# A row softmax on one core: the sixth load split in 14 and 2 rows, and the first store issued when the 14 rows have landed

## The chip, the cores and the metric

The kernel runs on one core of a Trainium2 chip. The metric is the device time of one execution in microseconds (us). The core has a vector engine (DVE), a scalar engine (ACT), a general engine (POOL) and a queue engine (SP), and 16 DMA engines that move data between the device memory (HBM) and the core's own memory. A DMA is issued by an instruction on the queue of ACT, SP or POOL, and each of the 16 DMA engines carries out its share of it. In the profile the DMA queue of ACT is called q10, that of SP q1 and that of POOL q0.

## The reference

The input is 16 x 1024 rows of 512 float32 numbers. Each row is divided by 0.5 and put through a softmax with the usual shift by the row's maximum:

```python
x_scaled = x / 0.5
x_max = np.max(x_scaled, axis=-1, keepdims=True)
exp_x = np.exp(x_scaled - x_max)
return exp_x / np.sum(exp_x, axis=-1, keepdims=True)
```

33.55 MB are read and 33.55 MB are written.

## The kernel before

The 16384 rows are cut in 8 chunks of 4 MB. A chunk is a tile of 128 partitions with 16 rows each, so one row index g (0 to 15) stands for 128 rows, and one partition's part of a chunk is 32 KB in one piece. Six chunk buffers exist (`BUFS`); chunks 6 and 7 reuse the buffers of chunks 0 and 1. All work is done in place.

A chunk is worked on in blocks (`BLOCKS`): chunk 0 in three (4, 4 and 8 rows), chunk 7 in two (8 and 8), all others whole. For each block there are four steps:

- `shift` (L74, L78): DVE takes the negative maximum of each row and doubles it. The result is the bias.
- `exponentials` (L104): ACT takes exp(2x + bias), one instruction for each row index, with the row's sum read out beside it.
- `scale_vector` (L121, L123): DVE inverts the sums and multiplies all row indices but the last eighth.
- `scale_scalar` (L134): ACT multiplies the last eighth (2 row indices of 16, 1 of 8).

The order on every engine is the order in which the program is written. The main loop goes over the blocks. For block i it issues the exponentials of block i+1, then the two scaling steps of block i, then the shift of block i+2, then the store of block i's chunk if the block is the chunk's last one. For chunk 1 the last two exponentials come after that store (function `rows`).

The loads (L65) of chunks 0 to 5 are all issued on ACT's queue at the start, one behind the other: chunk 0 in two pieces, the others whole. Chunks 6 and 7 are loaded on SP's queue. Load 6 waits until the store of chunk 0 has landed, load 7 until that of chunk 1 has; the last two rows of chunk 7 are loaded by POOL (L93), behind a small copy (L87) that waits for an exponential of chunk 5. All eight stores (L144) are issued on ACT's queue, each for a whole chunk of 4 MB. So loads 0 to 5 and all stores share one queue, and a store that is issued while loads are still under way lies behind them. At the end SP waits for all transfers.

Of the kernel before, what the change touches and what calls it, by code (L numbers as in the profile page):

```python
# [1 line left out]

# [4 lines left out]


@with_exitstack
def kernel(  # L10
    ctx: ExitStack,
    tc: tile.TileContext,
    x: bass.AP,
    out: bass.AP,
):
    nc = tc.nc
    fp32 = mybir.dt.float32
    P = nc.NUM_PARTITIONS
    AX = mybir.AxisListType.X
    EXP = mybir.ActivationFunctionType.Exp  # L20
    COPY = mybir.ActivationFunctionType.Copy
    MAX = mybir.AluOpType.max

    D = x.shape[-1]
    xf = x.flatten_outer_dims()
    of = out.flatten_outer_dims()
    N = xf.shape[0]

    G = 16
    C = N // (P * G)
    assert C * P * G == N
    xr = xf.rearrange("(c p g) d -> c p g d", p=P, g=G)
    outr = of.rearrange("(c p g) d -> c p g d", p=P, g=G)
    WHOLE = [(0, G)]
    LATE = 2
    LOADS = [[(0, 4), (4, G)]] + [WHOLE] * 6 + [[(0, G - LATE)]]
    BLOCKS = [[(0, 4), (4, 8), (8, G)]] + [WHOLE] * 6 + [[(0, 8), (8, G)]]  # L40
    STORES = [WHOLE] * 8
    BMAX = 16
    BUFS = 6

    data = ctx.enter_context(tc.tile_pool(name="data", bufs=BUFS))
    stats = ctx.enter_context(tc.tile_pool(name="stats", bufs=6))

    ctx.enter_context(tc.manual_schedule())


    chunks = {}
    blocks = [(c, lo, hi) for c in range(C) for lo, hi in BLOCKS[c]]
    n = len(blocks)
    biases, sums, recips = {}, {}, {}

    finished = []
    def load(c):
        if c < BUFS:
            chunks[c] = data.tile([P, G, D], fp32, name="xt")
        else:  # L60
            chunks[c] = chunks[c - BUFS]
        xt = chunks[c]
        queue = nc.scalar if c < BUFS else nc.sync
        for lo, hi in LOADS[c]:
            part = queue.dma_start(out=xt[:, lo:hi, :], in_=xr[c][:, lo:hi, :])  # L65
            finished.append(part.ins.name)

    def shift(i):
        c, lo, hi = blocks[i]
        if c not in chunks:  # L70
            load(c)
        b = hi - lo
        negmax = stats.tile([P, BMAX], fp32, name="negmax")
        nc.vector.tensor_reduce(  # L74
            negmax[:, 0:b], chunks[c][:, lo:hi, :], axis=AX, op=MAX, negate=True
        )
        biases[i] = stats.tile([P, BMAX], fp32, name="bias")
        nc.vector.tensor_scalar_mul(biases[i][:, 0:b], negmax[:, 0:b], 2.0)  # L78

    def load_last_rows(signal):
        seen = stats.tile([P, 1], fp32, name="seen", bufs=1)
        copied = nc.gpsimd.tensor_copy(out=seen, in_=signal)  # L87
        finished.append(copied.ins.name)
        c = C - 1
        to = chunks[c - BUFS][:, G - LATE : G, :]  # L90
        of_ = xr[c][:, G - LATE : G, :]
        for p0, p1 in ((P - 2, P), (0, P - 2)):
            part = nc.gpsimd.dma_start(  # L93
                out=to[p0:p1], in_=of_[p0:p1], max_dma_last_dim=4 * D
            )
            finished.append(part.ins.name)

    def exponentials(i, rows):
        c, lo, hi = blocks[i]
        if i not in sums:  # L100
            sums[i] = stats.tile([P, BMAX], fp32, name="sums")
        for g in rows:
            row = chunks[c][:, lo + g, :]
            nc.scalar.activation(  # L104
                out=row,
                in_=row,
                func=EXP,
                bias=biases[i][:, g : g + 1],
                scale=2.0,
                accum_out=sums[i][:, g : g + 1],  # L110
            )
            if c == BUFS - 1 and g == 10:
                load_last_rows(sums[i][:, g : g + 1])


    def scale_vector(i):
        c, lo, hi = blocks[i]
        b = hi - lo
        k = b - b // 8
        recips[i] = stats.tile([P, BMAX], fp32, name="recip")  # L120
        nc.vector.reciprocal(recips[i][:, 0:b], sums[i][:, 0:b])  # L121
        rows = chunks[c][:, lo : lo + k, :]
        last = nc.vector.tensor_mul(  # L123
            rows, rows, recips[i][:, 0:k].unsqueeze(2).broadcast_to((P, k, D))
        )
        if i == n - 1:
            finished.append(last.ins.name)

    def scale_scalar(i):
        c, lo, hi = blocks[i]  # L130
        b = hi - lo
        for g in range(b - b // 8, b):
            row = chunks[c][:, lo + g, :]
            last = nc.scalar.activation(  # L134
                out=row, in_=row, func=COPY, scale=recips[i][:, g : g + 1]
            )
            if i == n - 1:
                finished.append(last.ins.name)

    def store(i):  # L140
        c, _, end = blocks[i]
        for lo, hi in STORES[c]:
            if hi == end:
                part = nc.scalar.dma_start(  # L144
                    out=outr[c][:, lo:hi, :], in_=chunks[c][:, lo:hi, :]
                )
                if c < C - 1:
                    finished.append(part.ins.name)

    load(0)  # L150
    warm = stats.tile([P, 1], fp32, name="warm", bufs=1)
    nc.vector.memset(warm, 0.0)  # L152
    nc.scalar.activation(out=warm, in_=warm, func=EXP)  # L153
    for c in range(1, BUFS):
        load(c)

    shift(0)
    shift(1)

    def rows(i):  # L160
        c, lo, hi = blocks[i]
        cut = hi - lo - (2 if c == 1 else 0)
        return range(cut), range(cut, hi - lo)

    exponentials(0, rows(0)[0])
    for i in range(n):
        if i + 1 < n:
            exponentials(i + 1, rows(i + 1)[0])
        scale_vector(i)
        scale_scalar(i)  # L170
        if i + 2 < n:
            shift(i + 2)
        store(i)
        if i + 1 < n:
            exponentials(i + 1, rows(i + 1)[1])

    seen = nc.sync.nop()
    info = mybir.DependencyInfo(
        mybir.DependencyClass.Sync, mybir.DependencyReason.DATA
    )  # L180
    for name in finished:
        tc.add_manual_dep(seen.ins, name, info, reason="leaves one wait for the end")


# [1 line left out]
_INS = ['x']  # L186
_OUTS = [((16, 1024, 512), 'float32')]


# [23 lines left out]
```

## Time and profile before

| what | us |
|---|---|
| median of 3 runs | 162.73 (162.13 to 162.80) |
| the profiled execution | 162.08 |
| its span, first to last instruction | 160.2 |
| DVE busy | 134.6 |
| ACT busy | 102.2 |
| store of chunk 0 issued | 44.16 |
| store of chunk 1 issued | 59.02 |
| load 6 issued by SP | 72.61 |
| load 7 issued by SP | 88.3 |
| last multiply of DVE ends | 147.5 |
| last store issued | 147.56 |

All times inside the run count from the start of the span. The page's row named DMA gives the mean busy share of the 16 DMA engines in 40 slices of 4 us, a 9 being 90% or more; "busy" counts the time that packets took, so an engine with slow packets is busy too. In the groups of issues, the last number is the time from a DMA's issue to its landing, which includes the time that it lies behind others in its queue. In a table of stretches a line has the stretch, its length, the busy time of DVE, ACT and POOL with the number of instructions in brackets, the clock, the DMA share and the GB/s moved by the packets that started in it. In a timeline a line has start, duration, engine, line of the program, operation, tiles, and in square brackets the idle time before it and what ended it.

### The profile page before, as it was taken

Reading aid. Unit: us, or ns where it says so; the run is one execution under the profiler, and the core shown is the slowest. Engines: PE = TensorE matmul, PEld = TensorE weight load, DVE = VectorE, ACT = ScalarE, POOL = GpSimd, SP = SyncE. Lnnn points to the kernel's source line nnn. Section 1 sums busy time; section 2 is a strip of 40 time slices with the busy share of each in tenths; the row PEclk is TensorE's granted clock in tenths of the full one; section 3 lists DMA queues with packets and bytes.
Section 4 is the critical chain, followed back from the end, with each engine's and each line's share of the span. In section 5 each row is a group of like instructions: output and inputs, shape, how many; then the busy total and the mean of one; then the engine's idle time right before and its main releaser. Section 6 shows DMA issues by size and latency. Waiting matters only on the chain.

```text
span 160.2 us, 410 instructions
## 1 busy us (share of the span) xinstructions
DVE 134.6 (84%) x45; ACT 102.2 (64%) x273; POOL 1.9 (1%) x7
## 2 busy tenths in 40 slices
DVE  0607999999999999999999999999999999958000
ACT  3071549069989972998199909991899891690000
POOL 0000000000000000000000000040000000000000
DMA  5999999999999997999999999999999999999995
GB/s 184 470 401 507 401 393 499 417 393 468 442 401 442 466 401 303 475 393 434 475 401 417 475 409 417 444 459 394 428 456 436 397 466 450 393 442 466 401 401 245
DMA packets 2642, 67.13 MB, mean 419 GB/s; under 512 B 336, under 2 KB 336, under 8 KB 464
## 3 DMA queue, kind: packets, MB, share of 16 engines
q10 hardware_dynamic: 2160, 58.72, 86.0%
q1 hardware_dynamic: 288, 7.86, 11.4%
q0 software_dynamic: 192, 0.52, 0.8%
q14 instruction: 2, 0.02, 0.0%
HBM read 33.55 MB, written 33.55 MB: 419 GB/s over the span
## 4 chain that ended last, share of the span: by engine, by line
DVE 76%; DMA 7%; issue 5%; ACT 3%; ACTq 0%
DVE negmax L74 42%; DVE xt L123 32%; DMA xt<-in_x_dram 7%; ACT xt L104 3%; DVE bias L78 1%; DVE recip L121 1%; ACTq L65 0%
## 5 line engine op out<-in xcount | busy, mean ns | idle before, releaser
L104 ACT ACTIVATE xt<-xt,bias 128x512 f32<-128x512 f32 x128 | 90.4, 708 | 40.7 <-DVE bias L78 39.8
L74 DVE TENSOR_REDUCE negmax<-xt 128x16 f32<-128x8192 f32 (+2 forms) x11 | 69.9, 6353 | 9.5 <-DMA xt<-in_x_dram 9.5
L123 DVE TENSOR_TENSOR xt<-xt,recip 128x7168 f32<-128x7168 f32 (+2 forms) x11 | 62.0, 5637 | 0.4
L104 ACT ACTIVATION_READ_ACCUMULATOR xt<-xt,bias 128x1 f32 x128 | 23.9, 187 | 0.0
L134 ACT ACTIVATE xt<-xt,recip 128x512 f32<-128x512 f32 x15 | 9.9, 706 | 0.0
L121 DVE RECIPROCAL recip<-sums 128x16 f32<-128x16 f32 (+2 forms) x11 | 2.4, 219 | 1.8 <-ACT xt L104 1.8
L153 ACT ACT_TABLE_LOAD x1 | 1.3, 1283 | 1.6 <-PEq L197 1.6
L78 DVE TENSOR_SCALAR bias<-negmax 128x16 f32<-128x16 f32 (+2 forms) x11 | 1.9, 173 | 0.4
L93 POOL DMA_DIRECT2D xt<-in_x_dram x2 | 1.5, 741 | 0.5 <-issue 0.5
L87 POOL COPY seen<-sums 128x1 f32<-128x1 f32 x1 | 0.2, 184 | 103.7 <-ACT xt L104 103.7
L152 DVE MEMSET warm<- 128x1 f32 x1 | 0.1, 59 | 0.8 <-PEq L197 0.8
L153 ACT ACTIVATE warm<-warm 128x1 f32<-128x1 f32 x1 | 0.2, 202 | 0.0
L197 POOL MEMSET const-bfloat16-1.0<- 128x1 bf16 x1 | 0.1, 96 | 0.0
L197 POOL MEMSET const-uint8-127<- 128x1 uint8 x1 | 0.1, 96 | 0.0
L197 POOL MEMSET const-float32-0.0<- 128x1 f32 x1 | 0.1, 93 | 0.2 <-issue 0.2
L197 POOL MEMSET const-float32-1.0<- 128x1 f32 x1 | 0.1, 93 | 0.0
## 6 DMA issues: line engine op xcount, KB each, us to landing
out_dram<-xt ACTq DMA_DIRECT2D x8, 4096.0 KB, 24.9
xt<-in_x_dram ACTq DMA_DIRECT2D x5, 4096.0 KB, 39.5
xt<-in_x_dram SPq DMA_DIRECT2D x1, 4096.0 KB, 23.6
xt<-in_x_dram SPq DMA_DIRECT2D x1, 3584.0 KB, 26.4
xt<-in_x_dram ACTq DMA_DIRECT2D x1, 3072.0 KB, 11.7
xt<-in_x_dram ACTq DMA_DIRECT2D x1, 1024.0 KB, 4.8
xt<-in_x_dram POOLq DMA_DIRECT2D x1, 504.0 KB, 20.9
xt<-in_x_dram POOLq DMA_DIRECT2D x1, 8.0 KB, 9.6
```

The costliest lines, as they stand in the source:

```text
L74: nc.vector.tensor_reduce(negmax[:, 0:b], chunks[c][:, lo:hi, :], axis=AX, op=MAX, negate=True)
L78: nc.vector.tensor_scalar_mul(biases[i][:, 0:b], negmax[:, 0:b], 2.0)
L87: copied = nc.gpsimd.tensor_copy(out=seen, in_=signal)
L93: part = nc.gpsimd.dma_start(out=to[p0:p1], in_=of_[p0:p1], max_dma_last_dim=4 * D)
L104: nc.scalar.activation(out=row, in_=row, func=EXP, bias=biases[i][:, g : g + 1], scale=2.0, accum_out=sums[i][:, g : g + 1],)
L121: nc.vector.reciprocal(recips[i][:, 0:b], sums[i][:, 0:b])
L123: last = nc.vector.tensor_mul(rows, rows, recips[i][:, 0:k].unsqueeze(2).broadcast_to((P, k, D)))
L134: last = nc.scalar.activation(out=row, in_=row, func=COPY, scale=recips[i][:, g : g + 1])
L152: nc.vector.memset(warm, 0.0)
L153: nc.scalar.activation(out=warm, in_=warm, func=EXP)
L197: nc = _bacc.Bacc("TRN2", target_bir_lowering=False, num_devices=1)
```

## The change

The load of chunk 5, the sixth, is issued as two DMAs: rows 0 to 13 and rows 14 to 15. The store of chunk 0 is issued later in ACT's order: no longer after the scaling of chunk 0's last block, but in the next turn of the loop, just ahead of the store of chunk 1, so behind the exponentials of chunk 2 and the two scaling rows of chunk 1. It is given a wait for the first piece of load 5, the 14 rows. The two exponentials of chunk 1 that stood behind that store are issued with the other fourteen, ahead of chunk 0's scaling row. Nothing else is changed: DVE, POOL and SP have the same instructions in the same order.

```diff
     LATE = 2
-    LOADS = [[(0, 4), (4, G)]] + [WHOLE] * 6 + [[(0, G - LATE)]]
+    TAIL = 2
+    LOADS = [[(0, 4), (4, G)]] + [WHOLE] * 4 + [[(0, G - TAIL), (G - TAIL, G)], WHOLE, [(0, G - LATE)]]
...
     finished = []
+    released_by = {}
+    data_wait = mybir.DependencyInfo(
+        mybir.DependencyClass.Sync, mybir.DependencyReason.DATA
+    )
     def load(c):
...
             finished.append(part.ins.name)
+            released_by.setdefault(c, part.ins.name)
...
                 part = nc.scalar.dma_start(
                     out=outr[c][:, lo:hi, :], in_=chunks[c][:, lo:hi, :]
                 )
+                if c == 0:
+                    tc.add_manual_dep(
+                        part.ins, released_by[BUFS - 1], data_wait,
+                        reason="the first store starts where the loads end",
+                    )
...
     def rows(i):
         c, lo, hi = blocks[i]
-        cut = hi - lo - (2 if c == 1 else 0)
+        cut = hi - lo
         return range(cut), range(cut, hi - lo)
...
         if i + 2 < n:
             shift(i + 2)
-        store(i)
+        if blocks[i][0] == 1:
+            store(i - 1)
+        if blocks[i][0] > 0:
+            store(i)
```

## The prediction

> **What bounds the kernel now.** I read the page first (shares, DMA queues, chain of waits), then the stretches of equal length, then the waits of the SP queue, then the landing times and packet records at the two ends of the run. The page:
>
> ```profile
> DVE 134.6 (84%) x45; ACT 102.2 (64%) x273; POOL 1.9 (1%) x7
> ...
> DMA  5999999999999997999999999999999999999995
> ...
> q10 hardware_dynamic: 2160, 58.72, 86.0%
> q1 hardware_dynamic: 288, 7.86, 11.4%
> q0 software_dynamic: 192, 0.52, 0.8%
> ...
> HBM read 33.55 MB, written 33.55 MB: 419 GB/s over the span
> ...
> DVE 76%; DMA 7%; issue 5%; ACT 3%; ACTq 0%
> ```
>
> Two things are almost always busy: the 16 DMA engines (86.0 + 11.4 + 0.8 = 98% of the span) and DVE, which the chain puts at 76%. The chain follows DVE up to its last multiply; after it, at 147.47, comes the last store, issued at 147.56. So the question is whether that store finds the DMA engines free. The packet records say no for 15 of 16 engines: they end the store before at 148.85 to 149.33 and go on at once; one engine ran dry at 147.59 and began the last store at 148.40. So the DMA engines set the end, and DVE is under 1 us behind them. The rate in stretches of 9.7 us (the time of one 4 MB chunk; the last two columns are the DMA share and GB/s):
>
> ```profile
> 41.40:51.10 9.70, 9.63 (x4) 8.97 (x25) 0.00 (x0) 1.00 1.00 432
> 51.10:60.80 9.70, 9.70 (x2) 7.89 (x22) 0.00 (x0) 1.00 1.02 392
> 60.80:70.50 9.70, 9.63 (x4) 7.50 (x21) 0.00 (x0) 1.00 0.99 429
> 70.50:80.20 9.70, 9.63 (x5) 5.69 (x15) 0.00 (x0) 1.00 1.00 432
> ```
>
> The engines are busy throughout but move only 392 where 432 is usual: 9.7 x 40/432 = 0.9 us lost, in the stretch where the sixth load ends and the first store begins. The packets name it: 32 KB takes 1.21 to 1.22 us everywhere else; the last two packets of the sixth load on each engine take 1.2 to 1.8 and then 1.9 to 2.4. Its sixteen semaphore increments come at 61.66 to 62.78, those of the fifth load at 51.18 to 51.98; earlier loads are 9.71 apart, so 61.69 was due and the load is 1.09 late. Behind it in the same queue lies the first store, issued long before:
>
> ```profile
> 44.16 0.35 ACTq L144 DMA_DIRECT2D out_dram<-xt  x1
> ...
> 57.68 1.32 ACT L134 ACTIVATE xt<-xt,recip 128x512 f32<-128x512 f32 x2
> 59.02 0.35 ACTq L144 DMA_DIRECT2D out_dram<-xt  x1
> 62.79 0.17 DVE L78 TENSOR_SCALAR bias<-negmax 128x16 f32<-128x16 f32 x1
> ...
> 63.00 0.72 ACT L104 ACTIVATE xt<-xt,bias 128x512 f32<-128x512 f32 x1 [4.00 <-DVE bias L78]
> ```
>
> The reader sees here also that ACT, done at 59.4, idles 4.00 us before it can go on at 63.00. Who waits for that store is SP alone:
>
> ```profile
> SPq L65 <- DMA out_dram<-xt: 74.8, 2, 59.6
> ```
>
> **The change, part by part.** All against the profiled execution: span 160.2, time 162.08, so 1.9 us lie around the span. The median of the runs shown is 162.73, 0.65 above it; I apply the difference to the median.
>
> *One more load issue on ACT.* A load issue takes 0.48 us (median on that queue). It lies near 4.3, after the six others; ACT waits for its first bias until 8.09. Nothing, unless that 3 us cover went. The two-row packets are 4 KB: in the POOL load such a packet takes 0.159, so eight on each engine take 1.27, against 1.213 for the same 32 KB: +0.06, plus a 0.009 semaphore packet. Counted below.
>
> *Two exponentials of chunk 1 before the scaling row of chunk 0.* Two by 0.707 = 1.41 later for the scaling row: it would end at 43.43 + 1.41 + 0.70 = 45.5. The next bias comes at 46.34 in either case. Cost nothing; DVE's reciprocal of chunk 1 waits behind its own reduction (to 46.15) anyway. If DVE were 1 us earlier, this would show.
>
> *The first store moves behind the third chunk's exponentials and scaling rows.* ACT comes to it where it issued the second store before, at 59.02. Its issue (0.35) just moves, and the two stores now go one after the other.
>
> *The new wait, for the 14 rows.* The store's start decides. Undisturbed, the whole load is due at 61.69; the 14 rows 1.27 earlier, 60.42. From a landing to the issue that waits for it: 0.10 (first store landed 72.51, SP issued at 72.61). So the issue is at 60.52. From issue to first packet on a dry engine: 0.84 (147.56 to 148.40). First store packets at 61.36 on all engines. ACT stands still 59.02 to 60.52; behind the wait are the second store (60.87 to 61.22) and the exponentials of chunk 3, which need 63.00: 1.8 us of cover. The issue latency is seen once, on one engine of 16, so I bound it: below, 0 (the store's packets wait ready at the moment of issue); above, 1.02, the very first load (0.74 to 1.76). I take 0.84, the only store among these rows.
>
> *What goes, and what is late next.* The stretch should go, since no store lies behind the load while its last packets run; a dry gap comes instead: the 2 rows end about 60.5 to 61.3, so engines stand dry for 0 to 0.9 us. Before, the first store packets stood at 61.34 to 61.99 on fifteen engines (mean 61.70) and 62.48 on the last. At 61.36 for all, the mean engine gains 0.34, the latest of the fifteen 0.63, the earliest nothing. The engines are then full until the last store, so each carries its shift to the end. The engine of 62.48 is no matter: one engine has 1.3 us less to do later. Last packets end between 158.15 and 159.01; the end moves by 0.34 if the late engines at the end are average ones, by 0.63 if they are those late at 61.99. The POOL rows fall unevenly on the engines and mix the order, so I take 0.35.
>
> *SP's sixth-buffer chain.* The first store lands 1.0 us earlier (61.36 + 9.71 + 0.4 = 71.5), so load 6 is issued at 71.6 instead of 72.61. It landed at 96.2 and DVE wants it at 103.94; load 7 at 114.7, wanted at 120.56; POOL's rows at 126.5, wanted at 132.91. Nothing, with 6 us of cover. DVE's order is unchanged, its end stays at 147.47. Sum: -0.35 + 0.
>
> A rule that speaks against the change: the page "DMA: Bandwidth & Descriptors" of the Trainium skill (section "Anatomy of one DMA — SWDGE (gpsimd) path") sets about 2.0 us of fixed setup and completion on each DMA, for GpSimd's path. The rows above give 0.45 from last packet to landing on the slow engine, 0.10 and 0.84, 1.39 in all, from ACT's queue. By the rule the store would come 0.6 later and the sum would be +0.25, or 163.0.
>
> **The floor.** DVE sets how much can be gained: the last store cannot begin before 147.56 + 0.84 = 148.40, against a mean of 149.1 on the fifteen engines, and its issue to landing can shrink from 11.8 to 0.84 + 9.71 + 0.4 = 10.95. Gain at most 0.85.
>
> **The rivals.**
>
> *The stretch is not the queued store's (other side).* There is one turn from loads to stores in the run, so the trace cannot tell a store that waits in the ring from the turn itself. For it: nothing else in the queue has changed direction. Against it: 76 to 112, where loads and stores interleave on the same engines, runs at 432 to 433. If the last packets stay slow, the 14 rows land about 0.9 to 1.0 late, at 61.4, the store begins at 62.3 and the end is 0.3 to 0.6 later; if the turn also costs its 0.9 after the gap, 1.4. Middle 0.9: 163.6. It decides from a landing at 61.05 (store at 61.99) on. The same page (section "Two DMAs through the same engine are not ordered") says that an engine's read and write sides are separate queues and that descriptors are pipelined, which would let the store's reads run beside the load's last writes; no row shows the two sides apart.
>
> *The gap nearly closes.* The timed runs stand 0.65 above the profiled one; if that too lies in the stretch, or the store's packets are ready as the 2 rows end (60.7), the gain is the floor's 0.85: 161.9. Against it: the 0.84 seen.
>
> *It is hidden.* Shifts of the early engines are nil, and if those end last, nothing moves: 162.7.
>
> **How the numbers follow.** A measurement of this kernel can tell about 0.5%, 0.8 us, from no change. My forecast 0.50 (162.4; its own range 161.9 to 162.9), stretch stays 0.20, gap closes 0.20, hidden 0.10. Faster by over 0.5% (below 161.9): most of the closed gap, 0.17, and 0.09 of my own case, where the medians fall so: 0.26. Slower by over 0.5% (above 163.5): half of the staying stretch plus a worse issue latency, 0.17. The rest 0.57. The range leaves out the far part of the staying stretch and a little below the floor: 161.5 to 163.4.
>
> **What would show it.** In the changed profile: the stretch 51.1 to 60.8 back at 430 or more, and a dip in the DMA row just behind it; the fourteen rows landing near 60.4; both stores issued near 60.5 and 60.9; load 6 issued near 71.6; DVE's last multiply still ending at 147.5; the last store landing in less than 11.8. I am wrong if the 14 rows land after 61.0, if the first store's packets are slow, or if a DVE reduction waits for a load.

## The result and the profile after

The changed kernel is slower: 164.13 us at the median of 6 runs (164.09 to 164.39), against 162.17 for the kernel before (6 runs). The ratio is 1.0113, with a 95% interval of 1.0094 to 1.0132. The forecast was 162.4, and its range ended at 163.4. It was reckoned as 0.35 less than 162.73, the median of the three runs known then; against the 162.17 of these runs the change is +1.96 instead of -0.35. The profiled execution took 164.39, with a span of 162.4, 2.2 more than before.

The page of the changed kernel:

```profile
DVE 134.6 (83%) x45; ACT 102.1 (63%) x273; POOL 1.9 (1%) x7
...
DMA  5999899899998989999899999999999999999993
...
HBM read 33.55 MB, written 33.55 MB: 413 GB/s over the span
...
DVE 71%; issue 9%; DMA 7%; ACT 3%; ACTq 0%
```

DVE and ACT do the same work in the same time, and the same bytes move; only their rate over the span fell, from 419 to 413 GB/s. The stretches of 9.7 us say where (last column GB/s):

```profile
51.10:60.80 9.70, 9.70 (x2) 7.82 (x22) 0.00 (x0) 1.00 0.92 390
60.80:70.50 9.70, 9.63 (x4) 7.58 (x21) 0.00 (x0) 1.00 1.01 434
70.50:80.20 9.70, 9.63 (x5) 5.70 (x16) 0.00 (x0) 1.00 0.97 365
80.20:89.90 9.70, 9.70 (x2) 9.70 (x29) 0.00 (x0) 1.00 1.01 420
```

Before, the first three of these lines had 392, 429 and 432, and the last was:

```profile
80.20:89.90 9.70, 9.70 (x2) 9.70 (x29) 0.00 (x0) 1.00 1.00 432
```

The new loss lies at 70 to 80, ten microseconds after the place that was changed. The GB/s count packets by their start, so bytes can pass from one stretch to the next; the measure below is free of that. SP's queue and ACT's show what happens there:

```profile
60.70 0.84 ACTq L150 DMA_DIRECT2D out_dram<-xt  x2
62.72 0.17 DVE L84 TENSOR_SCALAR bias<-negmax 128x16 f32<-128x16 f32 x1
...
62.92 0.72 ACT L110 ACTIVATE xt<-xt,bias 128x512 f32<-128x512 f32 x1 [4.00 <-DVE bias L84]
```

```profile
71.97 17.50 SPq L70 DMA_DIRECT2D xt<-in_x_dram  x2
```

The first of these fences is the timeline, the second SP's alone (two loads merged: load 6 issued at 71.97, load 7 at 89.14). At 71.97 load 6 is issued, while the second store is running; before, its first packet came 3.45 after its issue (72.61 to 76.06), some three packets, and here it comes 4.9 after (76.88). In the packet records each engine's store packet that starts at 75.0, just ahead of the load's first, takes 1.56 to 2.15 instead of 1.21; four engines have one more store packet, of 2.45, and on some the load's first packet takes 1.75. From 79.5 on nearly all are at full speed. At 87 to 90, around the end of the second store, there is a smaller loss of the same kind.

For the experiments I use one measure, *lost time*: each packet's bytes are spread evenly over its duration, and each microsecond's total is held against the full 433 GB/s. Each figure is of one profiled execution; kernels whose first store is issued as before show 0.92 to 1.10 at the turn, so differences of 0.1 to 0.2 say little. Summed over three parts of the run:

| | at the turn, 56 to 66 | load 6 comes in, 66 to 84 | around the second store's end, 84 to 100 |
|---|---|---|---|
| before | 1.10 | 0.00 | 0.05 |
| after | 1.01 (mostly dry engines) | 1.21 | 0.48 |

The difference is -0.09 + 1.21 + 0.43 = 1.55. The last packet of the last engine ends 2.05 later (161.07 against 159.02); the remaining 0.5 is that the slow packets fall unevenly: the engines' last packets end within 0.9 us of each other before (158.15 to 159.01) and within 2.2 after (158.87 to 161.06), and the last one counts.

### The profile page after: what moved, and what is told of

Read it like the earlier page. It is cut to its first block, busy times and chain, and to the rows that moved or that the text cites. A ratio compares the mean times of both kernels' runs of the same rounds, so it can differ in the third digit from the quotient of the medians.

```text
span 162.4 us, 411 instructions
## 1 busy us (share of the span) xinstructions
DVE 134.6 (83%) x45; ACT 102.1 (63%) x273; POOL 1.9 (1%) x7
## 4 chain that ended last, share of the span: by engine, by line
DVE 71%; issue 9%; DMA 7%; ACT 3%; ACTq 0%
DVE negmax L80 41%; DVE xt L129 28%; DMA xt<-in_x_dram 7%; ACT xt L110 3%; DVE bias L84 1%; DVE recip L127 1%; ACTq L70 0%
```

## The experiments

"The turn" is the moment at which ACT's queue goes over from the loads to the first store. There were four theories on the second slow stretch when the experiments began: *paid once* (a cost that is due at the turn and only put off to load 6), *lockstep* (the wait lines up the 16 engines, so that they all turn to load 6 together), *date of load 6* (it comes 0.64 earlier than before), and *the split or the order*.

### Without the wait

The wait is taken out; split and order stay.

```diff
-                if c == 0:
-                    tc.add_manual_dep(
-                        part.ins, released_by[BUFS - 1], data_wait, ...
```

> The changed kernel without the wait for the 14 rows; split and order kept, so the first store is issued at about 59.0 behind the two-row load. The theories are on the changed kernel's second slow stretch, 75 to 79. Paid once (an engine whose stream turns with work already lying behind pays 1 to 1.5 us one time; a dry start only puts it off to load 6): slow packets again at 58 to 61.5, none at 75 to 79, time as before, 162.2 within 0.4. Lockstep (the dry start lines up the 16 engines, and they turn to load 6 together): the same, since no engine is dry and each keeps its own phase. Order or split alone at fault (two stores in one go, 4 KB packets): 164, with the slow stretch at 75 to 79 still there.

162.32, ratio 1.0003 (0.9994 to 1.0013): no slower than before. Lost time 1.08 at the turn, 0.00 at load 6, 0.04 later. The stretches where the changed kernel loses are at full rate again:

```profile
70.50:80.20 9.70, 9.63 (x5) 5.70 (x15) 0.00 (x0) 1.00 1.00 432
80.20:89.90 9.70, 9.70 (x2) 9.70 (x29) 0.00 (x0) 1.00 1.00 432
```

So neither the split into 14 and 2 rows nor the two stores' new place costs anything; the whole loss goes when the wait goes. One thing was not as expected, in the timeline of this run:

```profile
54.23 0.71 ACT L110 ACTIVATE xt<-xt,bias 128x512 f32<-128x512 f32 x1
54.35 0.35 ACTq L150 DMA_DIRECT2D out_dram<-xt  x1
```

The first store is issued at 54.35, not at 59.0: ACT's sequencer issues it while four exponentials and two scaling rows that stand ahead of it in the program have not begun.

### The wait ended earlier: 4 and 6 rows behind it

```diff
-    TAIL = 2
+    TAIL = 4
```

> The changed kernel with the load split in 12 and 4 rows, so the wait ends 1.3 us earlier: first store issued near 59.4, its packets ready near 60.3, while the loads still run to 60.5 to 61.4. No engine is dry. Paid once: some slow packets at the loads' end, 0.3 to 1 us, and none or little at 75 to 79; 161.9 to 162.4. Lockstep: no dry engine, each keeps its phase; no slow stretch at 75 to 79, and gain of the first stretch in part: 161.7 to 162.3. Wait as such at fault (stores issued late, whatever the state of the engines): 163.5 to 164.1.

162.82, ratio 1.0045 (1.0025 to 1.0064). No engine is dry and the turn costs nothing (0.09), yet the later losses are there, 0.98 and 0.58. The stretches of this run, from 51.1 on:

```profile
51.10:60.80 9.70, 9.70 (x2) 7.82 (x22) 0.00 (x0) 1.00 1.01 431
60.80:70.50 9.70, 9.63 (x4) 7.58 (x21) 0.00 (x0) 1.00 1.01 434
70.50:80.20 9.70, 9.63 (x5) 5.70 (x16) 0.00 (x0) 1.00 1.00 392
80.20:89.90 9.70, 9.70 (x2) 9.70 (x29) 0.00 (x0) 1.00 0.96 389
```

That is the forecast come true at its own place, 392 GB/s turned into 431, and taken back from ten microseconds later on. The engines begin the first store at 60.59 to 61.59, about as far apart as before (61.34 to 62.48), so the lockstep theory falls. A dry time is not needed either.

With `TAIL = 6`:

> The changed kernel with the load split in 10 and 6 rows: the ten rows land near 58, before ACT comes to the first store at 59.0, so the wait is there but ends ahead of it. If only the date of the issue counts: as without the wait, 162.0 to 162.5, slow stretch at 58 to 62 and none at 75 to 79. If the wait as such costs (ACT's queue, the semaphore): 163 or more.

162.60, ratio 1.0032 (1.0012 to 1.0052). The first store is issued at 58.02, as soon as the ten rows have landed, again ahead of ACT's exponentials. Lost time 0.11, 0.19, 0.55. The expectation took the date of issue for 59.0 and the result for that of the run without the wait; both were wrong, and it is not simply "before or behind ACT's turn".

### Load 6 held back

In the changed kernel load 6 gets a further wait, for an ACT instruction of a chosen date:

```diff
+            if c == BUFS:
+                tc.add_manual_dep(part.ins, later[0], data_wait, reason="load 6 starts later")
...
+            if c == 3 and g == 13:
+                later.append(done.ins.name)
```

With the fourteenth exponential of chunk 3, as shown:

> The changed kernel with load 6 held until the fourteenth exponential of chunk 3, so that it is issued near 72.9 instead of 71.97, as late as in the kernel before (72.61). Date of load 6 (it comes 0.64 too early in the stores' packets): slow stretch at 75 to 79 gone, 162.4 to 162.7. Paid once, and lockstep: it only moves by some 0.9 us, loss 1.3 to 1.7 us as before; 164.0 to 164.5.

Issue at 72.97; 163.95, ratio 1.0098 (1.0081 to 1.0114). Lost time at load 6 1.27. The theory of load 6's date falls: the load is issued later than in the kernel before (72.61) and still pays.

With chunk 2's last scaling row:

> The changed kernel with load 6 held until chunk 2's last scaling row is through, near 75.6, so 3.6 us later than in the changed kernel. If the loss belongs to the load's coming in: slow stretch at 79 to 83 instead of 75 to 79, of the same 1.0 to 1.3 us; 163.7 to 164.3. If it belongs to a place in the stores (the second store's middle, 75 to 79): it stays there, or goes: 162.5 to 163.

Issue at 75.78; 164.45, ratio 1.0148 (1.0105 to 1.0192). The slow stretch is now at 79 to 85, lost time 1.61. It goes where load 6 comes in; it is no matter of a place in the stores.

### Engines set apart

Two small copies are put behind the two-row load, one on eight engines and one on four of these eight. They are extra work, and their output is written over by the last store.

```diff
+        if i == 2:
+            for p0, p1, rows_ in ((0, 8, 15), (8, 12, 8)):
+                part = nc.scalar.dma_start(
+                    out=outr[C - 1][p0:p1, 0:rows_, :], in_=xr[0][p0:p1, 0:rows_, :]
+                )
```

> The changed kernel with two small copies (30 KB for each of 8 engines, 16 KB for each of 4, from the input to rows of the output that the last store writes later) behind the two-row load, so that 8 engines begin the first store near 61.6, 4 near 61.9 and 4 near 62.5: the engines' phases lie apart as before the change, and most of them still start dry. The copies add 0.3 us of work on average and up to 1.7 on four engines. Lockstep: no slow stretch at 75 to 79 (rate 425 or more), time 162.5 to 163.3. Paid once: the engines that started dry have it still, those behind a copy pay at the copies' end: rate at 70.5 to 80.2 below 400; 164 to 165.5.

165.19, ratio 1.0172 (1.0149 to 1.0196). The engines begin the first store at 61.63 to 63.33, wider than before the change, though eight of them still start within 0.1 us of each other. Lost time at load 6 0.92, later 0.88; 388 GB/s at 70.5 to 80.2. Lockstep falls a second time. The time holds the copies too, so only the rate is read here.

### A wait for the whole load

```diff
-    LOADS = ... [(0, G - TAIL), (G - TAIL, G)], WHOLE, ...
+    LOADS = ... WHOLE, WHOLE, ...
```

> The changed kernel with the load whole and the first store waiting for all of it: issue near 61.8, engines dry for about 2 us. What is now held: a store that lies in the queue early enough costs about 1.1 us once, at the turn; one that comes at the loads' end or later costs nothing there beside the dry time, and 1.0 to 1.3 us when load 6 comes in and 0.4 to 0.6 when load 7 does, however long the dry time was. Then: dry time 2.0 to 2.3, the later two losses 1.5 to 1.8 together, 164.9 to 165.5. If the later losses grew with the dry time (0 dry: 1.56, 0.9 dry: 1.69 so far), they would be 2.0 or more, 165.5 to 166.

165.46, ratio 1.0201 (1.0172 to 1.0229). Lost 2.06 at the turn, mostly dry engines, and 1.18 and 0.51 later. The later losses hardly grow with the dry time: 1.56 with none (4 rows), 1.69 with 0.84 us, the mean gap of the changed kernel's engines, and 1.69 with about 2.

### Loads and stores mixed at the turn

In the kernel before, load 5 goes to SP's queue and is held until an exponential of chunk 2.

```diff
-        queue = nc.scalar if c < BUFS else nc.sync
+        queue = nc.scalar if c < BUFS - 1 else nc.sync
...
+            if c == 2 and g == 0:
+                later.append(done.ins.name)
+                load(BUFS - 1)
...
```

> The kernel before with load 5 on SP's queue, held until chunk 2's first exponential (47.1), so that its packets come in near 50 and run beside load 4's end and the first store: no moment at which all engines turn from loads alone to stores alone. If the loss comes of that turn: no slow stretch at 50 to 70, nor at load 6; the end moves to the bound of DVE, 161.2 to 161.7. If every store that lies behind a load in its queue costs about 1 us, whatever runs beside it: a slow stretch at 49 to 52, 162.0 to 162.5. If a load's coming in beside stores costs: 163 or more.

163.61, ratio 1.0078 (1.0053 to 1.0104). The guess that mixing avoids the loss falls: 1.27 at 48 to 55, where load 5 comes in and the turn is at the same time. Load 6 then comes in near 76.5 and is free, but 0.96 more is lost at 85 to 89, around the second store's end, although the first store lay in the queue early and no engine had been dry. This loss is not explained. With the tenth exponential (`g == 9`):

> The same with load 5 held until chunk 2's tenth exponential (53.4), so that it comes in near 57, after ACT's queue has turned from load 4 to the first store at 51, which lies there since 44. If the early store pays about 1.1 us at the turn and nothing later: slow stretch at 49 to 52, none where load 5 comes in, 162.0 to 162.5. If the loss belongs to any load that comes in beside stores: a second slow stretch near 57, 163 or more.

162.45, ratio 1.0022 (1.0008 to 1.0035). Lost time 1.08, at the turn at 48 to 53; load 5 comes in at 57.05 and load 6 behind it on the same queue, both free. So a load that comes in beside stores is not dear in itself. It was free here after the turn had been paid.

### A small load first

In the changed kernel, 16 of the 128 partitions of the two-row piece are loaded on SP's queue, behind chunk 3's first exponential.

```diff
+    def load_few(after):
+        part = nc.sync.dma_start(
+            out=chunks[BUFS - 1][0:16, G - TAIL : G, :], in_=xr[BUFS - 1][0:16, G - TAIL : G, :]
+        )
...
```

> The changed kernel, but 16 of the 128 partitions of the two-row piece are loaded on SP's queue behind chunk 3's first exponential (63.7), one packet of 4 KB on each engine, so that a load of 64 KB comes in beside the first store near 67, before load 6 does at 76. Head start: the first load to come in pays, however small; slow stretch at 65 to 70 of about 1.2 us, and load 6 free; 164.0 to 164.5 in all. Each large load pays by itself: nothing at 65 to 70, the slow stretch at 75 to 79 as in the changed kernel; 164.0 to 164.5. Every load pays: both, 165.2 or more.

165.49, ratio 1.0196 (1.0179 to 1.0213). The 64 KB cost about 0.15 at 67 to 69 as they come in, and load 6 still pays 1.0 and 0.85 follows; the wait itself ended later here (issue at 61.20, 1.7 lost at the turn). A small load does not pay for the large one, so "the first load pays, however small" falls.

### A dry time after the turn has been paid

This is the test between one cost that moves and two costs. The control is the kernel before with load 6 held to the date of chunk 2's last scaling row:

> The kernel before with load 6 held until chunk 2's last scaling row, near 75.7, so that it comes in near 79. Control for the next run. If the early store's 1.1 us at the turn pays for all that follows: slow stretch at 58 to 62 as before, none at 79 to 84, 162.0 to 162.4. If load 6 was free before only because it came in before the third store was issued (75.64): a slow stretch of about 1.2 us at 79 to 84; 163.2 or more.

162.26, ratio 1.0003 (0.9994 to 1.0013). Turn 0.92, load 6 (issued 75.63, in at 79) 0.01.

Then the second store (`store(3)`: block 3 is chunk 1) is moved behind the thirteenth exponential of chunk 3 as well:

```diff
+            if c == 3 and g == 12:
+                store(3)
...
```

> The same, and the second store is issued later, behind the thirteenth exponential of chunk 3 (72.2), when the first has just ended: the engines stand dry for about 1.5 us near 71.5 to 73, and load 6 comes in near 79 as in the control. Head start (in the slow stretch at the turn each engine's reading gets ahead of its writing, and that head start is what later makes load 6 free; a dry time loses it): a slow stretch of 1.0 to 1.6 us at 78 to 84 besides the dry time; 164.5 to 165.3. Once per program (the first turn is paid once, whatever comes between): the dry time alone, 163.3 to 163.9.

162.53, ratio 1.0014 (1.0002 to 1.0026). This does not bear on the question: the second store was issued at 67.94, six exponentials early, the first was still running, and there was no dry time. With a wait for that exponential:

```diff
+                if c == 1:
+                    tc.add_manual_dep(part.ins, held_by[0], data_wait, ...)
```

> The kernel before with load 6 held to about 75.6 and the second store held until the thirteenth exponential of chunk 3 is through (72.2), by a wait this time, since ACT's sequencer issued it at 67.9 without one. The engines stand dry for 1 to 1.6 us near 71.5 to 73, and load 6 comes in near 79 (free in the control without the gap). Head start lost by a dry time: a slow stretch of 1.0 to 1.6 us at 78 to 84 besides the dry time, 164.3 to 165.5. The first turn is paid once, whatever comes between: the dry time alone, 163.2 to 163.9.

166.39, ratio 1.0258 (1.0243 to 1.0274). The stretches of the control and then of this run:

```profile
51.10:60.80 9.70, 9.70 (x2) 7.89 (x22) 0.00 (x0) 1.00 1.02 402
60.80:70.50 9.70, 9.63 (x4) 7.51 (x21) 0.00 (x0) 1.00 0.99 429
70.50:80.20 9.70, 9.63 (x5) 5.69 (x15) 0.00 (x0) 1.00 1.00 432
80.20:89.90 9.70, 9.70 (x2) 9.70 (x29) 0.00 (x0) 1.00 1.01 432
```

```profile
51.10:60.80 9.70, 9.70 (x2) 7.90 (x22) 0.00 (x0) 1.00 1.04 402
60.80:70.50 9.70, 9.63 (x4) 7.49 (x21) 0.00 (x0) 1.00 0.99 429
70.50:80.20 9.70, 9.63 (x5) 5.81 (x15) 0.00 (x0) 1.00 0.85 328
80.20:89.90 9.70, 9.70 (x2) 9.70 (x29) 0.00 (x0) 1.00 0.95 372
```

Up to 70.5 the two are alike, and the turn is paid in both (1.03 here). Then the engines are dry for 1.81 us at 71 to 73.2, and load 6, free in the control, is slow at 79 to 83 (1.17 in these bins) and 87 to 90 (0.42). After a dry time, then, a load that was free in the control is dear again, though the turn has been paid. The result lies above both expectations: dry time and slow packets make 3.4 of the 4.1 us by which the last packet is late, and the rest is again the uneven end (the last store lands on the 16 engines within 2.3 us, before within 0.9). DVE waits 0.37 us for a late load in this run and ends its last multiply at 147.9, which is too little to explain the 4.1 us.

### Two dates between

`TAIL = 8` and `TAIL = 10`:

> The changed kernel with the load split in 8 and 8 rows: first store issued near 56.6, between the 54.4 that cost 1.08 at the turn and nothing later and the 58.0 that cost 0.11 at the turn, 0.19 at load 6 and 0.55 at the second store's end. One cost that only moves: turn 0.3 to 0.9 and the later two together 0.1 to 0.5, sum 0.8 to 1.2; 162.1 to 162.5. Two separate costs with a window between their dates: turn under 0.3 and later under 0.3, 161.6 to 161.9, faster than both kernels.

> The same with 6 and 10 rows: first store issued near 55.3. One cost that only moves: turn 0.8 to 1.1, later 0 to 0.2; 162.0 to 162.4. Two separate costs with a window: as for 8 rows if the window begins before 55.3, else as the kernel without the wait.

162.28, ratio 1.0003 (0.9993 to 1.0013), and 162.27, ratio 1.0008 (0.9999 to 1.0017). With the runs above, in the order of the first store's issue:

| first store issued | kernel | at the turn | at load 6 | second store's end | ratio |
|---|---|---|---|---|---|
| 44.16 | before | 1.10 | 0.00 | 0.05 | 1 |
| 54.35 | without the wait | 1.08 | 0.00 | 0.04 | 1.0003 |
| 55.65 | 10 rows behind | 0.86 | 0.00 | 0.08 | 1.0008 |
| 57.17 | 8 rows behind | 0.80 | 0.06 | 0.14 | 1.0003 |
| 58.02 | 6 rows behind | 0.11 | 0.19 | 0.55 | 1.0032 |
| 59.63 | 4 rows behind | 0.09 | 0.98 | 0.58 | 1.0045 |
| 60.70 | after (2 rows) | 1.01, dry | 1.21 | 0.48 | 1.0113 |
| 61.80 | whole load | 2.06, dry | 1.18 | 0.51 | 1.0201 |

What leaves the turn comes up later. Beside the dry time the sums are 1.1 to 1.15 for the earliest stores, 0.85 to 1.0 in the middle, which is hardly less given the scatter, and 1.65 to 1.7 for the late ones. The smallest sum, with 6 rows, gives no shorter time, since its engines end less evenly (last packet of the last engine at 159.24 against 159.02 before). At none of these dates are both saved, and no version here beats the kernel before.

## Why the prediction was wrong, point by point

**What bounds the kernel** was right: DVE's last multiply still ends at 147.4, and every loss of the DMA engines shows in the end.

**The turn** was right to 0.4 us in its dates. Predicted and measured: 14 rows landed 60.42 and 60.63; first store issued 60.52 and 60.70; its first packets 61.36 and 61.56 to 61.71; load 6 issued 71.6 and 71.97. Its gain was not: 0.35 was forecast, and the lost time there fell by 0.09, since the dry engines cost nearly what the slow packets had. The slow packets of the last load are gone, as the forecast had it, and the first store lands at 71.84 instead of 72.51: a lead of 0.67 us on its last engine. The issue latency, taken from one engine's 0.84, was 0.86 to 1.01. By an estimate from the 2.0 us that the Trainium skill gives for GpSimd's path ("DMA: Bandwidth & Descriptors", "Anatomy of one DMA — SWDGE (gpsimd) path") the first packets would have come at 62.0; on ACT's queue the rows were the better price.

**Two exponentials, one more load issue, the wait on ACT** cost nothing, as said; without the wait the rest of the change runs at a ratio of 1.0003. One number was wrong without effect: ACT does not come to the store at 59.02. Without the wait its sequencer issued it at 54.35, with six of the program's operations ahead of it not begun.

**The step that failed** is "SP's sixth-buffer chain", with "Nothing, with 6 us of cover", and the sentence "The engines are then full until the last store, so each carries its shift to the end". I asked whether load 6 would be there in time for DVE. It was, and so were all others. I did not ask what its coming in does to the stores that it runs beside. That was free in the trace of before, and I took it for a property of mixed traffic (the 432 to 433 GB/s from 76 to 112, which I held against the rival). The runs show that it depends on what went before: load 6 was free where the first store had been issued by 55.7 and no engine had been dry since the turn, and it cost 0.9 to 1.6 where that store came from 59.6 on or the engines had run dry. The term that I set at zero measured 1.21 + 0.43, and 0.5 more by the uneven end; with the 0.09 won at the turn this is the 2.05 by which the last packet came later. None of the signs that the prediction named for being wrong came: the 14 rows landed before 61.0, the first store's packets took 1.21 to 1.25, and no DVE reduction waited anew. Two signs of being right stayed away: 51.1 to 60.8 was at 390, not 430, and the last store took 14.1 from issue to landing, not less than 11.8.

**The rivals.** "The stretch is not the queued store's" was wrong in its cause: the stretch went. Its price, 0.9 us and a time of 163.6, came near the result for the wrong reason, and its place was the turn, not load 6. "The gap nearly closes" happened at the turn with 4 rows, 431 GB/s and 0.09 lost, and was slower than before nevertheless; the floor set by DVE was never reached.

**What stays open.** The runs show that the cost moves with the date of the first store, that after a dry time load 6 is dear again, that neither the line-up of the engines nor the date of load 6 accounts for it, and that a small first load does not take its place. What lies behind it is only argued: in the slow stretch an engine's reading of the store's bytes may get ahead of its writing, and this head start may later cover the wait for load 6's first bytes from HBM. No record shows reading and writing apart. The Trainium skill ("DMA: Bandwidth & Descriptors", section "Two DMAs through the same engine are not ordered") says that an engine's read and write sides are separate queues, which would allow it; no run here shows it. Why the second store's end costs 0.4 to 0.9 in the same cases and with load 5 mixed in, and why the cost passes from the turn to load 6 between 57.2 and 59.6, was not settled either.

## What to carry to other kernels

A slow patch in a DMA-bound run can be tied to the smooth stretch behind it, so that the one goes with the other; before removing it, look at every later place where another stream comes in, and count what it would cost if the patch were gone. A transfer that joins has two prices: when it must be there, and what it does to those already running. Here the first store was best issued early, into a queue that was still busy; letting the engines run dry cost the dry time and about 1.7 us more.

## What the runs showed of the hardware that was not expected

- A load of 4 MB that joined a running store on another queue cost nothing where the first store had been issued by 55.7, the turn was over and no engine had been dry since. It cost 0.9 to 1.6 us where the first store came from 59.6 on or the engines had run dry, and 0.4 to 0.9 followed around the second store's end. With load 5 mixed in at the turn, load 6 was free and 0.96 was lost at the second store's end all the same.
- ACT's sequencer issues a DMA that has no wait ahead of the work: at 54.35 with four exponentials and two scaling rows not begun, at 67.94 with one exponential running and five not begun. Program order on ACT alone did not set the date of a store; a wait did. The page "Advanced Engine Details and Errata" of the Trainium skill (section "Sequencer Loop") has the sequencer push engine instructions into a queue and read on, which agrees with these two dates.
- From a DMA's landing to the first packet of one that waits for it: 0.07 + 0.86 us on ACT's queue (60.63, 60.70, 61.56).
